# Four of seven Strassen products summed in one PSUM bank: a new product order and a fifth weight buffer in the first half of a fused transformer block

## The chip, the cores and the metric

The kernel runs on one core of one Trainium2 chip. The metric is the device time of one execution in microseconds; the time before is the median of three runs. Five engines work side by side, each with its own queue of instructions: TensorE (PE in the profile, its weight loads PEld), VectorE (DVE), ScalarE (ACT), GpSimd (POOL) and SyncE (SP), which issues most transfers. TensorE writes into PSUM, which has eight banks of 128 x 512 floats; VectorE and ScalarE read the banks from there.

## The reference

One layer on `x` of 2048 tokens by 1024 features, in float32:

```python
h    = rmsnorm(x, norm_g)
proj = einsum('bsd,de->bse', h, w_in)     # 1024 -> 4*512 + 4*512 + 2*1024 = 6144 columns
q, k, v, z_att, gb, gc, u, z_conv, g_att, g_conv = split(proj)
att    = chunked_rel_attention(q, k, v, rel_bias)      # 8 heads of 64; own chunk of 64 and 8 before
y_att  = (att * silu(z_att)) @ w_att_out
y_conv = (gb * causal_conv3(gc * u) * silu(z_conv)) @ w_conv_out
m   = sigmoid(g_att) * y_att + sigmoid(g_conv) * y_conv
x   = x + m @ w_out
out = rmsnorm(x, final_norm_g)
```

The change lies in `proj`, the large product of 2048 x 1024 by 1024 x 6144.

## The kernel before

**Tiles.** The tokens are taken in two halves of 1024 (two blocks of 512 columns each; the kernel holds everything transposed, features on partitions). The 6144 output columns are 24 pairs of 128-column tiles. One pair of one half is a 2 x 2 block product (output tiles by token blocks, with the 1024 features cut in two), and it is made by the Strassen-Winograd scheme with seven block products in place of eight. They bear the numbers 1 to 7. The tuple `ORDER` (L36) sets in which order they are made: 1, 2, 6, 5, 7, 4, 3. Each product sums over four tiles of 128 features, and each of these is done in three passes (`passes`, L132 to L137), because weights and activations are split into a high and a low part: high by high (L135), high by low (L136), low by high (L137). A product is therefore twelve matmuls of 128 x 512, into one PSUM bank.

**Operands.** `operand_steps` (L348 to L362) makes the seven activation operands of a half, four tiles each: an add for operand 6 (L354), a subtract for 4 (L356) and for 5 (L360), or the block itself, and then a split (`split_pair`, L125 to L130): ScalarE casts the high part (L128), VectorE subtracts it to get the low part (L129). In the names of the profile `t40h` is the high part of operand 4, tile 0. `operand` (L375 to L399) makes the weight operand of one product in the same way: up to three sums on VectorE (L390 to L396), then `split_into` with ScalarE's cast (L122) and VectorE's subtract (L123). Its tile `wc` comes from the pool `wr` of four buffers. The first half also stores each one to DRAM; the second half loads it back. Weight operands are made two products ahead of their use in the first half and three ahead in the second (`ahead`, L753). The raw weights are loaded a pair ahead (`load_raw`, L370 to L373, called at L749).

**Sums of the products.** The results of a pair are four blocks, c11, c12, c21, c22. With `u` and `v` as running sums, the code at L774 to L801 does this after each product, reading its bank once or twice: ScalarE copies product 1 into `u` (L776); VectorE makes c11 = u + product 2 (L780), u += product 6 (L784), v = u + product 5 (L787), c22 = v + product 7 (L791), u += product 7 (L792), c21: u += product 4 (L796), c12: v += product 3 (L800). That is seven adds and one copy per pair. Scratch tiles `u`, `v`, `c` come from the pool `ep` of ten buffers. Each finished block goes to a handler of its kind (L402 to L499): a gate gets a tanh on ScalarE (L404) and is stored; a q or k block is split again, ScalarE's cast `hi` (L410) and VectorE's subtract (L411); a v block is transposed by TensorE into a bank `vt` (L433) and cast out of it by ScalarE (`vst`, L440) and VectorE; z and the short convolution have their own.

**PSUM.** The pool `ps_d` has three banks; products, plain products, `vt` and the spread norm `rb` take turns in it. The other five belong to the attention's pools `ps_s`, `ps_t` and `ps_m`, opened at the start of the program (L99).

**Order of the work.** The first three pairs of the first half (`PLAIN`) are done plainly, in twelve accumulations L686 to L727, while x is still being normalised: their banks are `ps_p`, and `scaled` (L636 to L639) frees a bank by multiplying it with 1/rms (L638) on VectorE. The order of that part is the order in which it is written. Then the main loop (L741 to L822) goes through the list of (pair, product) steps `seq`. From there on a scheduler arranges each engine's instructions by their dependences and their places in the program, so that they do not stand simply in the order of the code. The last pairs of the first half and the first of the second are interleaved product by product (`together`, L584); beside them the second half's activation operands are made. Early in the second half `wo_steps` (L549 to L578) prepares the output weights `xw` on VectorE (L570 to L574). After that the attention of all heads (L177 to L259) is interleaved with the rest of the second half, and the two closing projections follow.

Of the kernel before, what the change touches and what calls it, by code (L numbers as in the profile page):

```python
# [34 lines left out]

ORDER = (1, 2, 6, 5, 7, 4, 3)  # L36
NPAIR = 24
# [3 lines left out]
def block_kernel(ctx, tc, xb, xt, wp_in, wy, wo, bias, ng, fg, cw, cb, out):  # L41
# [89 lines left out]

    def passes(ps, w, rhs, cs=slice(0, CH), first=True, last=True):  # L132

        for k, (rh, rl) in enumerate(rhs):
            nc.tensor.matmul(ps, lhsT=w[:, 0, k, :], rhs=rh[:, cs], start=(first and k == 0), stop=False)  # L135
            nc.tensor.matmul(ps, lhsT=w[:, 0, k, :], rhs=rl[:, cs], start=False, stop=False)  # L136
            nc.tensor.matmul(ps, lhsT=w[:, 1, k, :], rhs=rh[:, cs], start=False, stop=(last and k == len(rhs) - 1))  # L137

# [156 lines left out]
    def inverse(y, make):  # L295

        ps = dbank("rb")
        spread(ps, y, 4)
        rb = make("rb")
        nc.scalar.copy(rb, ps)  # L300
        return rb
# [98 lines left out]


    def ev_gate(i, d):  # L402
        def ev(g, c, t):
            nc.scalar.activation(t, t, AF.Tanh, scale=0.5)  # L404
            nc.scalar.dma_start(gate_d[i][d][g], t)
        return ev

    def parts(t):
        hi = e("hi")
        nc.scalar.copy(hi.bitcast(F32R), t)  # L410
        nc.vector.tensor_sub(t.bitcast(F32R), t, hi)  # L411
        return hi, t
# [15 lines left out]
    def ev_v(pr):  # L428
        def ev(g, c, t):
            def turn():  # L430
                ps = dbank("vt")
                for b in range(4):
                    nc.tensor.transpose(out=ps[:, b * P:(b + 1) * P], in_=t[:, b * P:(b + 1) * P], identity=ident)  # L433
                defer(0, lambda: split(ps))
# [28 lines left out]
    def conv_pair(b):  # L463
# [21 lines left out]
        def ev_cu(g, c, t):  # L485
            if c in got:
                conv(c, got.pop(c), t)
            else:
                got[c] = t

# [96 lines left out]

    both = [(i, k) for i in (6, 5, 7, 4, 3) for k in range(2)]
    ending = [(1, 0), (2, 0), (6, 0), (1, 1), (2, 1), (6, 1), *both[2:]]
# [151 lines left out]
    for s, (p, i) in enumerate(seq):  # L741
        half = p // NPAIR
        n = names.index(p)
        if due and due[0] <= s:
            due.pop(0)
            next(turned)
        if half == 0 and i == 1 and n + 1 < NPAIR:
            for k in range(2):
                load_raw(names[n + 1], k)  # L749
        elif i == 1 and n in (NPAIR, *range(NPAIR + 2, NPAIR + 1 + PLAIN)):  # L750
            for k in range(2):
                load_raw(names[max(n, NPAIR + 1) + 1], k)
        ahead = 3 if half else 2  # L753
        while nw < min(len(seq), s + ahead + 1):
            operand(*seq[nw])
            nw += 1
        if half == 0 and len(built) < 7 and s:
            built.append(next(steps))
        if n == 5 and i == 1:
# [3 lines left out]
            x1 = norm_steps(1)  # L763
        if half == 0 and 8 <= n < 22 and i in (2, 5, 4):
# [4 lines left out]
        ps = dbank("ps_d")  # L769
        passes(ps, wops.pop((p, i)), [ops[half, i, j] for j in range(4)])  # L770
        tick()
        ev = evs[p % NPAIR]
        g0, g1 = 2 * half, 2 * half + 1
        if i == 1:  # L774
            u = e("u")
            nc.scalar.copy(u, ps)  # L776
            uv[p] = [u, None]
        elif i == 2:
            t = e("c11")
            nc.vector.tensor_add(t, uv[p][0], ps)  # L780
            ev[0](g0, 0, t)
        elif i == 6:
            u = uv[p][0]
            nc.vector.tensor_add(u, u, ps)  # L784
        elif i == 5:
            v = uv[p][1] = e("v")
            nc.vector.tensor_add(v, uv[p][0], ps)  # L787
        elif i == 7:
            u, v = uv[p]
            t = e("c22")  # L790
            nc.vector.tensor_add(t, v, ps)  # L791
            nc.vector.tensor_add(u, u, ps)  # L792
            ev[1](g1, 1, t)
        elif i == 4:
            u = uv[p][0]
            nc.vector.tensor_add(u, u, ps)  # L796
            ev[1](g0, 0, u)
        else:
            v = uv.pop(p)[1]
            nc.vector.tensor_add(v, v, ps)  # L800
            ev[0](g1, 1, v)  # L801
        if n == NPAIR - 1:
# [9 lines left out]
        if n == NPAIR + 1 + PLAIN and i == 3:  # L812
            for _ in mixed:
                pass
            first.close()
            att = ExitStack()
            ab = attention(att.enter_context(tc.tile_pool(name="ab", bufs=1, side="right")))
# [303 lines left out]
```

## Time and profile before

| | |
|---|---|
| runs of before | 1537.36, 1541.26, 1545.34 us; median 1541.26 |
| profiled execution | 1537.43 us, span of the trace 1535.7 us |
| mean granted TensorE clock | 0.995 |
| memory traffic | 408.32 MB by DMA, 266 GB/s; 251.67 MB read from HBM, 155.19 MB written |

How to read the profile: it is one execution, and `L135` is line 135 of the kernel. Busy time counts an instruction from its start to its end; since matmuls are pipelined and their ends are modelled, the pace of TensorE is read from the distance of starts, or from how many matmuls a stretch holds. In the timeline a row is start, duration, engine, line, operation, output and inputs, and in brackets the idle time before it and what ended that. In a group's row stand busy time, mean nanoseconds of one, and the idle time before the group with its main releaser. The waits are rows of engine, waiting tile and line, releaser, then microseconds in all, their count, and the longest. Row pieces such as `x119` are counts.

### The profile page before, as it was taken

To read this page: it belongs to the slowest core of one execution; us is meant where nothing else is said; L and a number is where in the kernel's file an instruction comes from. 1 tells how busy PE (TensorE), PEld (TensorE's weight loads), DVE (VectorE), ACT (ScalarE), POOL (GpSimd) and SP (SyncE) were. 2 spreads that over 40 slices of the span, in tenths; PEclk is the share of its full clock that TensorE was granted. 3 is DMA by queue.
4 is the path that set the end of the run, shared out by engine and by line. 5 is a ranking of instruction groups with operands and counts; after the bars stand their busy time and mean duration, and the time that the engine had idled before them with its cause. 6 is when DMAs were issued, how large, how long until landed. Compare 5 with 4: busy or idle time off the path is not lost.

```text
span 1535.7 us, 21757 instructions
## 1 busy us (share of the span) xinstructions
PE 1493.8 (97%) x7300; PEld 1247.1 (81%) x7300; DVE 1108.6 (72%) x2140; ACT 714.5 (47%) x1314; POOL 164.0 (11%) x310
## 2 busy tenths in 40 slices
PE   8899999999999999999999999999999999999997
PEld 6678888888777778888888888888888888888885
DVE  7977789797668774666666767676755578777787
ACT  6353353443335333555566656666665223423252
POOL 0000000000000001233222223222220000010000
PEclk9999999999999999999999999999999999999999
DMA  5288999988988984999898777878888944877442
GB/s 206 76 287 310 343 350 326 360 324 290 334 301 277 318 315 149 336 342 337 299 295 278 236 259 235 264 240 267 293 273 300 337 116 163 297 253 234 149 157 110
DMA packets 168750, 408.32 MB, mean 266 GB/s; under 512 B 21056, under 2 KB 41536, under 8 KB 168640
## 3 DMA queue, kind: packets, MB, share of 16 engines
q1 hardware_dynamic: 137152, 316.74, 59.4%
q0 software_dynamic: 22272, 73.42, 14.6%
q10 hardware_dynamic: 9216, 16.78, 2.9%
q8 instruction: 58, 0.95, 0.3%
q14 instruction: 52, 0.43, 0.1%
HBM read 251.67 MB, written 155.19 MB: 265 GB/s over the span
## 4 chain that ended last, share of the span: by engine, by line
PE 79%; DVE 10%; DMA 5%; issue 3%; ACT 3%; POOL 0%; SPq 0%; ACTq 0%; DVEq 0%; POOLq 0%
PE ps_d L137 19%; PE ps_d L135 19%; PE ps_d L136 19%; PE ps_w L953 6%; PE ps_d L953 4%; PE po L228 4%; PE ps_s L190 3%; PE ps_t L210 3%; DMA wc<-wc 1%; DMA vv<-v 1%; DVE ptl L216 1%; DMA xw<-wo 1%; DVE ps_s L196 1%; DVE xs L304 1%; ACT pr L200 1%
## 5 line engine op out<-in xcount | busy, mean ns | idle before, releaser
L158 POOL DMA_DIRECT2D q<-q x128 | 66.9, 528 | 675.2 <-DVE wc L123 598.4
L200 ACT ACTIVATE pr<-ps_s,nmax 128x640 f32<-128x640 f32 (+4 forms) x128 | 93.4, 730 | 96.9 <-DVE nmax L196 96.2
L196 DVE CUSTOM_DVE_ANT_0 ps_s<-ps_s,bs 128x640 f32<-128x640 f32 (+4 forms) x128 | 95.3, 744 | 53.9 <-PE ps_s L190 53.2
L122 ACT CAST wc<-wraw 128x512 fp32r<-128x512 f32 x120 | 73.4, 620 | 105.9 <-PE ps_d L137 80.1
L202 ACT ACTIVATE pr<-pr,rs 128x640 f32<-128x640 f32 (+4 forms) x128 | 97.8, 764 | 27.4 <-DVE rs L201 27.3
L190 PE MATMUL ps_s<-kk,q 128*128 128x320 f32 (+1 forms) x448 | 98.0, 335 | 2.8 <-ACT pr L200 2.6
L216 DVE TENSOR_TENSOR ptl<-ps_t,pth 128x640 fp32r<-128x640 f32 (+4 forms) x128 | 94.2, 736 | 7.5 <-ACT pth L215 6.9
L137 PE MATMUL ps_d<-mid,wy 128*128 128x512 f32 x256 | 99.6, 389 | 0.0
L135 PE MATMUL ps_d<-mid,wy 128*128 128x512 f32 x256 | 99.6, 389 | 0.0
L136 PE MATMUL ps_d<-mid,wy 128*128 128x512 f32 x256 | 99.6, 389 | 0.0
L215 ACT CAST pth<-ps_t 128x640 fp32r<-128x640 f32 (+4 forms) x128 | 80.1, 626 | 41.3 <-PE ps_t L210 40.3
L123 DVE TENSOR_TENSOR wc<-wraw,wc 128x512 fp32r<-128x512 f32 x120 | 81.8, 686 | 10.1 <-ACT wc L122 9.9
L210 PE MATMUL ps_t<-ident,pr 128*128 128x128 f32 x560 | 83.9, 276 | 1.0 <-DVE ptl L216 0.5
L228 PE MATMUL po<-pth,vv 128*128 128x256 f32 x336 | 79.1, 271 | 2.6 <-DMA vv<-v 2.5
L228 PE MATMUL po<-ptl,vv 128*128 128x256 f32 x336 | 78.1, 281 | 0.0
L190 PEld LDWEIGHTS ps_s<-kk,q 128*128 128x128 f32 x448 | 67.0, 190 | 7.6 <-ACT pr L200 7.2
L210 PEld LDWEIGHTS ps_t<-ident,pr 128*128 128x128 f32 x560 | 63.3, 141 | 11.1 <-DVE ptl L216 2.0
L953 PE MATMUL ps_w<-wo,lefth 128*128 128x512 f32 x224 | 69.9, 393 | 0.0
L228 PEld LDWEIGHTS po<-pth,vv 128*128 128x128 f32 x336 | 63.8, 190 | 6.0 <-issue 2.6
L228 PEld LDWEIGHTS po<-ptl,vv 128*128 128x128 f32 x336 | 63.8, 190 | 2.4 <-DVE ptl L216 0.2
L137 PEld LDWEIGHTS ps_d<-mid,wy 128*128 128x128 f32 x256 | 48.1, 188 | 10.1
L136 PEld LDWEIGHTS ps_d<-mid,wy 128*128 128x128 f32 x256 | 48.1, 188 | 10.0
(383 smaller groups left out, 4174.2 us busy)
## 6 DMA issues: line engine op xcount, KB each, us to landing
wc<-wc SPq DMA_DIRECT2D x294, 512.0 KB, 4.8
wraw<-wp_in SPq DMA_DIRECT2D x54, 512.0 KB, 6.1
q<-q POOLq DMA_DIRECT2D x128, 128.0 KB, 4.9
gl<-gate SPq DMA_DIRECT2D x64, 256.0 KB, 3.2
mid<-mid SPq DMA_DIRECT2D x64, 256.0 KB, 5.3
wor<-wo SPq DMA_DIRECT2D x56, 256.0 KB, 5.2
bs<-bias POOLq DMA_DIRECT2D x32, 320.0 KB, 7.5
gate<-c ACTq DMA_DIRECT2D x34, 256.0 KB, 5.2
```

The lines of the kernel that those rows point to most:

```text
L123: nc.vector.tensor_sub(w[:, 1], src, w[:, 0].bitcast(F32))
L135: nc.tensor.matmul(ps, lhsT=w[:, 0, k, :], rhs=rh[:, cs], start=(first and k == 0), stop=False)
L136: nc.tensor.matmul(ps, lhsT=w[:, 0, k, :], rhs=rl[:, cs], start=False, stop=False)
L137: nc.tensor.matmul(ps, lhsT=w[:, 1, k, :], rhs=rh[:, cs], start=False, stop=(last and k == len(rhs) - 1))
L190: nc.tensor.matmul(ps[:, i, :m], lhsT=q[s][:, g * P:(g + 1) * P], rhs=kk[:, k1 - n + i * m:k1 - n + (i + 1) * m], start=(s == 0), stop=(s ...
L196: nc.vector.tensor_tensor_reduce(out=view, in0=view, in1=bv, scale=-0.125, scalar=3.0e38, op0=ALU.add, op1=ALU.min, accum_out=nmax)
L200: nc.scalar.activation(out, view, AF.Exp, bias=nmax, scale=-1.0, accum_out=rs)
L202: nc.scalar.activation(pr[:, :n], pr[:, :n], AF.Identity, scale=rs)
L210: nc.tensor.transpose(out=ps[:, j * P:(j + 1) * P], in_=pr[:, j * P:(j + 1) * P], identity=ident)
L216: nc.vector.tensor_sub(lo[:, js, qs], src, hi[:, js, qs].bitcast(F32))
L228: nc.tensor.matmul(ps[:, (g0 + a) * P:(g0 + b) * P], lhsT=vv[:, g0 + j, :], rhs=s[:, j, a * P:b * P], start=(i == 0 and s is pt[0]), stop= ...
L953: nc.tensor.matmul(ps, lhsT=lhs[:, gs], rhs=rhs, start=(not onto and j == n == 0), stop=(j == 3 and n == 2), skip_group_check=onto)
```

## The change

The change rearranges the first half's Strassen products and the PSUM banks they use.

- `ORDER` becomes 1, 2, 6, 7, 4, 5, 3, in both halves.
- In the first half, products 1, 6, 5 and 3 of a pair go into one shared bank (pool `ps_c`, two banks). Product 1 starts it; 6, 5 and 3 add onto what is there (`onto`). Between them ScalarE copies the bank out: after product 1 and after product 6 into a `u`, after product 5 into `v`. After product 3 the bank itself is c12, and it is passed to the handler as it is. Product 7 has a pool of its own, `ps_h`, of two banks, which is held until it is read twice. Products 2 and 4 stay in `ps_d`. VectorE's adds are now four per pair: c11 after 2, u after 7, c21 after 4, and v += product 7 after 5, which makes c22. ScalarE's copies are three.
- The second half keeps a bank per product and sums in the new order: u after 6, w = u + product 7, c21 = w + product 4, then w and u each plus product 5, u plus product 3.
- The weight pool `wr` has five buffers in place of four, the scratch pool `ep` eight in place of ten. Weight operands are made three products ahead in both halves.
- The attention's pools are opened only when the attention begins; until then their five banks are `ps_m` (one), `ps_c` and `ps_h`. Two of the v transposes and `rb` use `ps_m`.
- In the first half the steps of neighbouring pairs interleave: 6, 7, 4, 5 of a pair, then products 1 and 2 of the next pair, then 3.
- The raw weights' load is issued after `operand` of the step, and the small work (norm steps of the second half, bias) after the product, not ahead of it.

```diff
-ORDER = (1, 2, 6, 5, 7, 4, 3)
+ORDER = (1, 2, 6, 7, 4, 5, 3)
...
-    wr = pool("wr", 4)
-    ep = pool("ep", 10)
+    wr = pool("wr", 5)
+    ep = pool("ep", 8)
     ps_d = pool("ps_d", 3, space=PSUM)
     banks = ExitStack()
-    ps_s, ps_t, ps_m = (banks.enter_context(tc.tile_pool(name=name, bufs=1, space=PSUM)) for name in ("ps_s", "ps_t", "ps_m"))
+    ps_m = banks.enter_context(tc.tile_pool(name="ps_m", bufs=1, space=PSUM))
+    ps_c = banks.enter_context(tc.tile_pool(name="ps_c", bufs=2, space=PSUM))
+    ps_h = banks.enter_context(tc.tile_pool(name="ps_h", bufs=2, space=PSUM))
...
-    def passes(ps, w, rhs, cs=slice(0, CH), first=True, last=True):
+    def passes(ps, w, rhs, cs=slice(0, CH), first=True, last=True, onto=False):
...
+            nc.tensor.matmul(ps, lhsT=w[:, 0, k, :], rhs=rh[:, cs], start=(first and not onto and k == 0), stop=False, skip_group_check=onto)
...
+    def own(src):
+        return src if src.space != PSUM else e("c12")
+
+    def copied_out(src):
+        t = own(src)
+        if t is not src:
+            nc.scalar.copy(t, src)
+        return t
...
-    def parts(t):
-        hi = e("hi")
-        nc.scalar.copy(hi.bitcast(F32R), t)
-        nc.vector.tensor_sub(t.bitcast(F32R), t, hi)
+    def parts(src):
+        hi, t = e("hi"), own(src)
+        nc.scalar.copy(hi.bitcast(F32R), src)
+        nc.vector.tensor_sub(t.bitcast(F32R), src, hi)
...
-                ps = dbank("vt")
+                ps = bank("vt") if g < 2 else dbank("vt")
...
-    seq = [(p, i) for p in mid0 for i in ORDER]
+    seq = [(mid0[0], 1), (mid0[0], 2)]
+    for p, nxt in zip(mid0, names[PLAIN + 1:]):
+        seq += [*((p, i) for i in (6, 7, 4, 5)), (nxt, 1), (nxt, 2), (p, 3)]
...
+        ahead = 3
+        while nw < min(len(seq), s + ahead + 1):
+            operand(*seq[nw])
+            nw += 1
         if half == 0 and i == 1 and n + 1 < NPAIR:
             for k in range(2):
                 load_raw(names[n + 1], k)
-        ahead = 3 if half else 2
-        while nw < min(len(seq), s + ahead + 1):
-            operand(*seq[nw])
-            nw += 1
...
+        onto = half == 0 and i in (6, 5, 3)
+        if onto:
+            ps = uv[p][0]
+        elif half == 0 and i in (1, 7):
+            ps = (ps_c if i == 1 else ps_h).tile([P, CH], F32, tag="b", name="ps_c")
+        else:
+            ps = dbank("ps_d")
+        passes(ps, wops.pop((p, i)), [ops[half, i, j] for j in range(4)], onto=onto)
...
+        elif half == 0:
+            if i == 6:
+                u = uv[p][2] = e("u")
+                nc.scalar.copy(u, ps)
+            elif i == 7:
+                u = uv[p][2]
+                nc.vector.tensor_add(u, u, ps)
+                uv[p][1] = ps
+            elif i == 4:
+                u = uv[p][2]
+                nc.vector.tensor_add(u, u, ps)
+                ev[1](g0, 0, u)
+            elif i == 5:
+                v = e("v")
+                nc.scalar.copy(v, ps)
+                nc.vector.tensor_add(v, v, uv[p][1])
+                ev[1](g1, 1, v)
+            else:
+                uv.pop(p)
+                ev[0](g1, 1, ps)
```

What this does to the queues is seen at two places. The first is ScalarE's queue at the last q and k pair of the first half. Before, with `wc_4059`, `wc_4078` and `wc_4099` the weights of products 7, 4 and 3, and `hi_4119` the cast of c22, which is finished after product 7:

```order
L122 CAST wc_4034<-s1_4007 128x512
L410 CAST hi_4056<-c11_4054 128x512
L122 CAST wc_4059<-wraw_3836 128x512
L410 CAST hi_4119<-c22_4116 128x512
L122 CAST wc_4078<-wraw_3836 128x512
L122 CAST wc_4099<-wraw_3834 128x512
```

After, at the same pair, with `wc_3942`, `wc_3969` and `wc_3989` the weights of products 7, 4 and 5, `u_3940` the copy of product 1, `hi_3985` the cast of the previous pair's c12 out of the shared bank, and `u_4007` the copy after product 6:

```order
L124 CAST wc_3942<-wraw_3756 128x512
L793 COPY u_3940<-ps_c_3922 128x512
L124 CAST wc_3969<-wraw_3756 128x512
L124 CAST wc_3989<-s1_3911 128x512
L422 CAST hi_3965<-u_3940 128x512
L422 CAST hi_3985<-ps_c_3758 128x512
L803 COPY u_4007<-ps_c_3922 128x512
```

The cast of product 4's weights stood behind a cast of the sum that product 7 completes; it now stands between the copy of product 1 and the weights of product 5.

The second place is VectorE's queue at the start, between the multiplies by 1/rms that free the plain products' banks. Before, `t50l` to `t53l` are the low parts of activation operand 5:

```order
L638 TENSOR_TENSOR c_1108<-ps_p_1006,rb_925 128x512
L360 TENSOR_TENSOR t1_1141<-xs_547,xs_533 128x512
L129 TENSOR_TENSOR t50l_1144<-t1_1141,t50h_1143 128x512
L360 TENSOR_TENSOR t1_1147<-xs_547,xs_533 128x512
L129 TENSOR_TENSOR t51l_1150<-t1_1147,t51h_1149 128x512
L360 TENSOR_TENSOR t1_1153<-xs_547,xs_533 128x512
L129 TENSOR_TENSOR t52l_1156<-t1_1153,t52h_1155 128x512
L360 TENSOR_TENSOR t1_1159<-xs_547,xs_533 128x512
L129 TENSOR_TENSOR t53l_1162<-t1_1159,t53h_1161 128x512
L638 TENSOR_TENSOR c_1165<-ps_p_1063,rb_852 128x512
```

After, from the same multiply on, with the low parts of operands 7 and 4 and, in the last row, the split of the weights of the first Strassen product:

```order
L654 TENSOR_TENSOR c_1108<-ps_p_1006,rb_925 128x512
L131 TENSOR_TENSOR t70l_1142<-xs_544,t70h_1141 128x512
L131 TENSOR_TENSOR t71l_1146<-xs_544,t71h_1145 128x512
L131 TENSOR_TENSOR t72l_1150<-xs_544,t72h_1149 128x512
L131 TENSOR_TENSOR t73l_1154<-xs_544,t73h_1153 128x512
L654 TENSOR_TENSOR c_1157<-ps_p_1063,rb_852 128x512
L358 TENSOR_TENSOR xs_539<-xs_539,xs_533 128x512
...
L131 TENSOR_TENSOR t43l_1203<-xs_539,t43h_1202 128x512
L654 TENSOR_TENSOR c_1206<-ps_p_1116,rb_852 128x512
L125 TENSOR_TENSOR wc_1210<-wraw_558,wc_1210 128x512
```

Four bare splits now stand between the first and the second multiply, where four subtracts and four splits stood; four subtracts and splits stand between the second and the third, and the first weights' split comes behind those. Lines 124, 125, 130, 131, 422, 654, 793, 803 and 814 of the changed kernel are the lines 122, 123, 128, 129, 410, 638, 776 and the two new copies after products 6 and 5.

More of the change, by code (lines that the diff above doesn't have):

```diff
@@ L130, in split_pair @@
         return hi, lo
-    def passes(ps, w, rhs, cs=slice(0, CH), first=True, last=True):
+    def passes(ps, w, rhs, cs=slice(0, CH), first=True, last=True, onto=False):
         for k, (rh, rl) in enumerate(rhs):
-            nc.tensor.matmul(ps, lhsT=w[:, 0, k, :], rhs=rh[:, cs], start=(first and k == 0), stop=False)
-            nc.tensor.matmul(ps, lhsT=w[:, 0, k, :], rhs=rl[:, cs], start=False, stop=False)
-            nc.tensor.matmul(ps, lhsT=w[:, 1, k, :], rhs=rh[:, cs], start=False, stop=(last and k == len(rhs) - 1))
+            nc.tensor.matmul(ps, lhsT=w[:, 0, k, :], rhs=rh[:, cs], start=(first and not onto and k == 0), stop=False, skip_group_check=onto)
+            nc.tensor.matmul(ps, lhsT=w[:, 0, k, :], rhs=rl[:, cs], start=False, stop=False, skip_group_check=onto)
+            nc.tensor.matmul(ps, lhsT=w[:, 1, k, :], rhs=rh[:, cs], start=False, stop=(last and k == len(rhs) - 1), skip_group_check=onto)
     def attention(ab):
@@ L295, in inverse @@
     def inverse(y, make):
-        ps = dbank("rb")
+        ps = bank("rb")
         spread(ps, y, 4)
@@ L488, in ev_cu @@
             else:
-                got[c] = t
+                got[c] = copied_out(t)
         def gated(g, c, t):
@@ L746, in block_kernel @@
             next(turned)
+        if i == 1 and n in (NPAIR, *range(NPAIR + 2, NPAIR + 1 + PLAIN)):
+            for k in range(2):
+                load_raw(names[max(n, NPAIR + 1) + 1], k)
+        ahead = 3
+        while nw < min(len(seq), s + ahead + 1):
+            operand(*seq[nw])
+            nw += 1
         if half == 0 and i == 1 and n + 1 < NPAIR:
@@ L763, in block_kernel @@
             x1 = norm_steps(1)
-        if half == 0 and 8 <= n < 22 and i in (2, 5, 4):
+        ev = evs[p % NPAIR]
+        g0, g1 = 2 * half, 2 * half + 1
+        onto = half == 0 and i in (6, 5, 3)
[6 more added lines that the diff above has]
+        passes(ps, wops.pop((p, i)), [ops[half, i, j] for j in range(4)], onto=onto)
+        tick()
+        if i == 1:
+            u = e("u")
+            nc.scalar.copy(u, ps)
+            uv[p] = [ps, None, u]
+        elif i == 2:
+            u = uv[p][2]
+            t = u if half == 0 else e("c11")
+            nc.vector.tensor_add(t, u, ps)
+            ev[0](g0, 0, t)
+        elif half == 0:
+            if i == 6:
+                u = uv[p][2] = e("u")
+                nc.scalar.copy(u, ps)
+            elif i == 7:
[3 more added lines that the diff above has]
+            elif i == 4:
+                u = uv[p][2]
+                nc.vector.tensor_add(u, u, ps)
[8 more added lines that the diff above has]
+                ev[0](g1, 1, ps)
+        elif i == 6:
+            u = uv[p][2]
+            nc.vector.tensor_add(u, u, ps)
+        elif i == 7:
+            w = uv[p][1] = e("w")
+            nc.vector.tensor_add(w, uv[p][2], ps)
+        elif i == 4:
+            t = e("c21")
+            nc.vector.tensor_add(t, uv[p][1], ps)
+            ev[1](g0, 0, t)
+        elif i == 5:
+            _, w, u = uv[p]
+            nc.vector.tensor_add(w, w, ps)
+            nc.vector.tensor_add(u, u, ps)
+            ev[1](g1, 1, w)
+        else:
+            u = uv.pop(p)[2]
+            nc.vector.tensor_add(u, u, ps)
+            ev[0](g1, 1, u)
+        if half == 0 and 8 <= n < 22 and i in (2, 7, 4):
             next(x1, None)
@@ L768, in block_kernel @@
             nbias += 1
[L769 to L801, printed above, removed]
         if n == NPAIR - 1:
@@ L815, in block_kernel @@
             first.close()
+            banks.close()
+            ps_s, ps_t, ps_m = (banks.enter_context(tc.tile_pool(name=name, bufs=1, space=PSUM)) for name in ("ps_s", "ps_t", "ps_mm"))
             att = ExitStack()
```

15 lines of the change are left out of this document (7 added, 8 removed).

## The prediction

> **What bounds the kernel now.** I read the page first, for the busy shares and the chain of work that ended last.
>
> ```profile
> PE 1493.8 (97%) x7300; PEld 1247.1 (81%) x7300; DVE 1108.6 (72%) x2140; ACT 714.5 (47%) x1314; POOL 164.0 (11%) x310
> PE 79%; DVE 10%; DMA 5%; issue 3%; ACT 3%; POOL 0%; SPq 0%; ACTq 0%; DVEq 0%; POOLq 0%
> ```
>
> TensorE is the bound. The change removes no matmul, so all it can win is time in which TensorE does not run at its pace. Next I read the busy time by stretches (columns: TensorE, weight load, VectorE, ScalarE, GpSimd, each with its count, granted clock, DMA share).
>
> ```profile
> 50.00:90.00 40.00, 30.81 (x119) 24.06 (x118) 36.11 (x59) 18.88 (x33) 0.00 (x0) 0.91 0.34 111
> 120.00:400.00 280.00, 280.00 (x1241) 231.91 (x1240) 228.46 (x418) 112.27 (x201) 0.00 (x0) 1.00 0.89 329
> 400.00:440.00 40.00, 36.12 (x160) 28.77 (x158) 25.62 (x41) 11.89 (x24) 0.00 (x0) 1.00 0.84 303
> 440.00:480.00 40.00, 39.62 (x183) 32.08 (x184) 28.47 (x52) 17.08 (x36) 0.00 (x0) 1.00 0.95 319
> 480.00:520.00 40.00, 34.92 (x143) 27.32 (x142) 38.75 (x65) 20.82 (x37) 0.00 (x0) 0.96 0.80 283
> 560.00:600.00 40.00, 38.02 (x168) 31.16 (x168) 25.01 (x39) 14.63 (x24) 0.24 (x1) 1.00 0.43 157
> 720.00:1160.00 440.00, 435.67 (x2545) 380.47 (x2544) 300.30 (x607) 273.84 (x476) 114.62 (x214) 1.00 0.82 268
> ```
>
> From 120 to 400 us, which holds most pairs of the first half, TensorE is never idle: 1241 matmuls in 280 us, one every 0.2256 us, so a product of twelve takes 2.71 us and 40 us hold 177 matmuls. What the other stretches lack against 177 is the loss: 58 matmuls from 50 to 90 (13.1 us), 17 from 400 to 440 (3.9), 34 from 480 to 520 (7.7), 9 from 560 to 600 (2.0); 440 to 480 has 0.4 us of idle time. Together 27.1 us are lost in the first half and its transition. The list of TensorE's waits from 50 to 600 us says for whom.
>
> ```profile
> PE ps_p L135 <- DVE c L638: 9.2, 3, 4.6
> PE ps_d L137 <- DVE wc L123: 5.5, 4, 3.1
> PE ps_d L135 <- ACT wc L122: 3.5, 3, 1.9
> PE ps_d L135 <- DVE u L784: 2.0, 1, 2.0
> ```
>
> And the timeline of TensorE, at those waits:
>
> ```profile
> 60.35 0.47 PE L135 MATMUL ps_p<-rawh,w 128*128 128x512 f32 x1 [2.48 <-DVE c L638]
> ...
> 76.25 0.80 PE L135 MATMUL ps_p<-rawh,w 128*128 128x512 f32 x1 [4.61 <-DVE c L638]
> ...
> 77.27 0.63 PE L137 MATMUL ps_p<-rawh,w 128*128 128x512 f32 x1
> 77.70 0.63 PE L135 MATMUL ps_p<-rawh,w 128*128 128x512 f32 x1
> ...
> 85.59 0.50 PE L135 MATMUL ps_p<-rawh,w 128*128 128x512 f32 x1 [2.09 <-DVE c L638]
> ...
> 87.31 0.63 PE L137 MATMUL ps_p<-rawh,w 128*128 128x512 f32 x1
> 87.73 0.63 PE L135 MATMUL ps_p<-rawh,w 128*128 128x512 f32 x1
> ...
> 92.79 0.39 PE L135 MATMUL ps_d<-t10h,wc 128*128 128x512 f32 x1
> ...
> 414.08 0.50 PE L135 MATMUL ps_d<-t40h,wc 128*128 128x512 f32 x1 [1.95 <-ACT wc L122]
> ...
> 436.21 0.50 PE L137 MATMUL ps_d<-t40h,wc 128*128 128x512 f32 x1 [1.53 <-DVE wc L123]
> ...
> 491.23 0.50 PE L135 MATMUL ps_d<-t70h,wc 128*128 128x512 f32 x1 [1.31 <-ACT wc L122]
> ...
> 501.29 0.50 PE L137 MATMUL ps_d<-t40h,wc 128*128 128x512 f32 x1 [3.14 <-DVE wc L123]
> ...
> 565.13 0.47 PE L135 MATMUL ps_d<-t40h,wc 128*128 128x512 f32 x1 [1.98 <-DVE u L784]
> ```
>
> So only eight places matter, and at most of them a weight split comes late, not a sum. After two of the start's waits matmuls follow each other at 0.43 instead of 0.23 us for a while: the start's 13.1 us are 9.2 of waiting and 3.9 of such slow stretches.
>
> **Part by part: the adds and copies.** In the first half each pair loses three of its seven VectorE adds and gains two ScalarE copies.
>
> ```profile
> L787 DVE TENSOR_TENSOR v<-u,ps_d 128x512 f32<-128x512 f32 x21 | 14.4, 685 | 13.0 <-PE ps_d L137 13.0
> L776 ACT COPY u<-ps_d 128x512 f32<-128x512 f32 x21 | 12.2, 583 | 12.6 <-PE ps_d L137 12.2 <-ACT v L404 0.4
> ```
>
> By 0.69 and 0.58 us that is 3 x 0.69 = 2.1 us per pair off VectorE, about 43 us over 21 pairs, and 21 x 2 x 0.58 = 24 us onto ScalarE. VectorE has 51 us to spare from 120 to 400, and TensorE never waits there: both terms are nothing in that stretch. The cover for the copies is that products 6, 5 and 3, which add into the shared bank, each come two products (5.4 us) after the one whose sum is copied out; a copy of 0.58 us fits unless ScalarE is held up for more than 4.8 us. For the first pair there is only one product between 1 and 6. If the cover is gone, TensorE stands for the excess.
>
> **The start.** VectorE's and ScalarE's rows there:
>
> ```profile
> 75.52 0.68 DVE L638 TENSOR_TENSOR c<-ps_p,rb 128x512 f32<-128x512 f32 x1
> ...
> 78.14 0.69 DVE L129 TENSOR_TENSOR t50l<-t,t50h 128x512 fp32r<-128x512 f32 x1 [1.35 <-ACT t50h L128]
> ...
> 80.17 0.69 DVE L129 TENSOR_TENSOR t51l<-t,t51h 128x512 fp32r<-128x512 f32 x1 [0.74 <-ACT t51h L128]
> ...
> 84.85 0.68 DVE L638 TENSOR_TENSOR c<-ps_p,rb 128x512 f32<-128x512 f32 x1
> ```
>
> Between the multiply that frees one plain bank (75.52) and the next (84.85) stand four rounds of subtract, cast, split for operand 5, 2.03 us each (78.14 to 80.17). In the new order four bare splits of operand 7 stand there, so the second multiply starts at 76.2 + 1.35 of waiting for a cast + 4 x 0.69 = 80.3 and ends at 81.0: the 2.09 us wait at 85.59 goes, and with it half of the slow stretches, 4.0 us together. The 2.48 and 4.61 us waits hang on rows that stay. But four such rounds (operand 4) now stand ahead of the split of the first product's weights: 81.0 + 8.1 + a multiply and the split, 1.4, is 90.5, where TensorE, which began that product at 92.79, is 4.0 us earlier, at 88.8. It waits 1.7 us (bounds 0 and 4.0). Term: -2.3 us, between -4.0 and 0.
>
> The trace throttles after a wait of 2.09 us. [...]
>
> **From 400 to 480.** The wait at 414.08 is made by queue order, not by load:
>
> ```profile
> 412.17 0.69 DVE L791 TENSOR_TENSOR c<-v,ps_d 128x512 f32<-128x512 f32 x1
> 412.89 0.62 ACT L410 CAST hi<-c 128x512 fp32r<-128x512 f32 x1 [7.02 <-DVE c L791]
> 413.41 1.66 ACT L122 CAST wc<-wraw 128x512 fp32r<-128x512 f32 x3
> ```
>
> ScalarE holds the cast of product 4's weights behind the cast of a finished sum that waits for product 7, the one just before: 0.69 + 0.62 + 0.62 = 1.93, and 1.95 was waited. In the new ScalarE order that weight cast stands behind product 1's copy, three products ahead of need: gone. The wait at 436.21 (an add of product 7 ahead of the split) goes with the fifth buffer's extra product of lead, 2.71 us. In their place I see in the new order three tight spots at the v pairs: a weight cast behind the cast out of a transpose that TensorE does just before, a weight cast behind a copy that waits for such a transpose, and a split behind three weight sums.
>
> ```profile
> 439.71 0.37 ACT L440 CAST vst<-vt 128x256 fp32r<-128x256 f32 x1 [5.03 <-PE vt L433]
> ```
>
> The first is 0.37 + 0.62 plus a quarter of a microsecond at the low part, 1.3; the second 0.58 + 0.62 = 1.2; the third about 0.4. Term: 4.3 lost before, 2.9 after, -1.4 us (bounds -4.3 and +1.5, if each doubles).
>
> **From 480 to 520.** Here VectorE is full (38.75 of 40 us), since the second half's operands are made beside the last two pairs, and the splits come late. Two pairs lose six adds, 4.1 us of VectorE; weights come a product earlier; operand 5 is needed two products later. That exceeds the 3.14 and 1.31 us waits. I leave 1.0 us: -6.7 us (bounds -7.7 and 0, as the order in this crowded place is new).
>
> **From 560 to 600.** VectorE stood 4.6 us before a row of the output weights, with the add that frees a bank behind it:
>
> ```profile
> 562.25 0.69 DVE L570 TENSOR_TENSOR xw<-xw 128x512 f32<-128x512 f32 x1 [4.62 <-DMA xw<-wo]
> ```
>
> The new order spreads these rows between other adds, but the load can be as late: half of it, -1.0 us (bounds -2.0 and +1.0).
>
> **The rest at nothing.** The raw weights' load is issued after the splits of the step and behind them in SP's queue. It now has four products (10.8 us) where five were, and lands in 6.1 us at the median:
>
> ```profile
> wraw<-wp_in SPq DMA_DIRECT2D x38, 512.0 KB, 6.1
> ```
>
> Two scratch tiles fewer can make a copy wait for a store; stores hide behind the same two products. The small work that is moved behind the product (norm steps, bias) has no reader near. The second half keeps its counts, and from 720 to 1160 only 4.3 us are idle, so order changes there are worth within 4 us either way; I take 0.
>
> **Sum.** -2.3 - 1.4 - 6.7 - 1.0 = -11.4 us. The profiled execution took 1537.4 us, so 1526 for one like it; the median of the runs is 3.8 us higher at 1541.3, and from it 1530.
>
> **The rivals.** *The copies become the wait.* Sharing a bank makes TensorE wait wherever ScalarE is late with a copy. For it: the 7.02 us for which ScalarE stood before a cast at 412.89, and that q, k and v pairs keep such casts, now behind adds of product 4 and ahead of the copy of product 5. Against it: those casts wait for a product already done two products before the bank is needed. It decides once a copy ends later than 5.4 us after its product. If two points in each of the six q, k and v pairs then cost the 1.95 us of 414.08, that is 23.4 us, +12.0 net: 1553. [...]
>
> *The waits only move.* They came from the order in which weight casts and sums stand in ScalarE's and VectorE's queues, which is drawn up anew; new tight spots could return what 400 to 600 gives. Only the start's term is left: 1539. For it: three such spots are visible already. Against it: all weights now come one product earlier.
>
> *More goes than I count.* If the start loses its wait for weights too (-4.0), and 400 to 480 (-4.3), 480 to 520 (-7.7) and 560 to 600 (-2.0) lose everything: -18.0, 1523, or below if the slow stretch after 76.25 also shrinks. For it: the fifth buffer works at each of these places.
>
> **How the numbers follow.** 0.52 for the forecast (its own range 1523 to 1537), 0.15 for more, 0.24 for waits that move, 0.09 for late copies. A measurement of this kernel can tell about 0.5%, 7.7 us, from no change: 1533.6. Of the forecast's chance 0.37 lies below that. Faster: 0.37 + 0.15 = 0.52. Slower takes most of the last rival, 0.07. The same is 0.41. The range reaches from 1517, under the third rival, to 1546, over the second with the second half's 4 us and some scatter of the runs; it leaves out most of the first.
>
> **What would show it.** Right: full TensorE from 120 to 400, no wait at the product 4 that waited at 414.08, at least 165 matmuls where 480 to 520 had 143, a start with two waits for plain banks instead of three and one for the first weights. Wrong: waits of TensorE at products 6, 5 or 3 for ScalarE's copies; weight waits of over 5 us in sum between 400 and 600; a second half with more than 8 us idle from 720 to 1160.

## The result and the profile after

The changed kernel takes 1525.52 us (median of five runs, 1523.16 to 1526.19), beside 1540.23 us for the kernel before (five runs); the ratio is 0.9904 with a 95% interval of 0.9876 to 0.9932. A second series, with more runs of both on one chip, gave 1524.42 and 1537.15 us: 0.9911 (0.9893 to 0.9928). The forecast was 1530, 11 us less; the runs say 13 to 15 us less, and between the two profiled executions (1537.43 and 1525.53 us) it is 11.9.

The page of the profile after, busy shares and the chain of work that ended last:

```profile
PE 1490.2 (98%) x7300; PEld 1246.4 (82%) x7300; DVE 1071.2 (70%) x2077; ACT 732.5 (48%) x1358; POOL 163.6 (11%) x310
PE 83%; DVE 8%; issue 3%; DMA 3%; ACT 2%; POOL 0%; SPq 0%; ACTq 0%; DVEq 0%; POOLq 0%
```

VectorE has 63 instructions fewer, three in each of the 21 pairs, and ScalarE 44 more: the 42 copies, and two of finished blocks whose handler needs them out of the bank. That is 37 us off VectorE and 18 onto ScalarE, less than the 43 and 24 that had been counted. The chain's share on VectorE and on DMA went to TensorE. Next the busy time by the stretches that were shown of before (TensorE, weight load, VectorE, ScalarE, GpSimd, each with its count, granted clock, DMA share and rate).

```profile
50.00:90.00 40.00, 31.60 (x131) 24.81 (x129) 32.36 (x54) 17.49 (x31) 0.00 (x0) 0.96 0.33 108
120.00:400.00 280.00, 280.00 (x1241) 231.90 (x1240) 206.83 (x377) 126.26 (x233) 0.00 (x0) 1.00 0.94 337
400.00:440.00 40.00, 38.93 (x177) 31.75 (x176) 21.53 (x37) 13.18 (x27) 0.00 (x0) 1.00 0.80 284
440.00:480.00 40.00, 38.75 (x180) 31.75 (x179) 27.17 (x50) 22.04 (x46) 0.00 (x0) 1.00 0.90 309
480.00:520.00 40.00, 37.13 (x155) 29.69 (x154) 34.23 (x58) 18.93 (x35) 0.00 (x0) 0.96 0.89 315
560.00:600.00 40.00, 40.00 (x178) 33.15 (x177) 21.12 (x33) 13.98 (x23) 7.57 (x14) 1.00 0.50 152
720.00:1160.00 440.00, 438.01 (x2567) 383.83 (x2567) 299.91 (x608) 279.25 (x480) 111.85 (x209) 1.00 0.83 268
```

From 120 to 400 us nothing changed for TensorE: 1241 matmuls in both profiles, with 22 us less of VectorE and 14 more of ScalarE beside them. The gains lie where the prediction had put the losses. TensorE's idle time from 400 to 480 falls from 4.3 to 2.3 us; 480 to 520 holds 155 matmuls in place of 143, still 22 short of full; 560 to 600 is full. The second half, from 720 to 1160, has 2.0 us of idle time in place of 4.3. What TensorE still waits for shows in its timeline from 50 to 600 us; these are the rows with a wait, not neighbours, and in the end the row behind the last of them:

```profile
59.99 0.47 PE L137 MATMUL ps_p<-rawh,w 128*128 128x512 f32 x1 [2.49 <-DVE c L654]
75.60 0.50 PE L137 MATMUL ps_p<-rawh,w 128*128 128x512 f32 x1 [4.32 <-DVE c L654]
89.98 0.50 PE L137 MATMUL ps_c<-t10h,wc 128*128 128x512 f32 x1 [1.60 <-ACT wc L124]
435.99 0.50 PE L137 MATMUL ps_d<-t20h,wc 128*128 128x512 f32 x1 [1.07 <-ACT wc L124]
467.86 0.50 PE L137 MATMUL ps_c<-t10h,wc 128*128 128x512 f32 x1 [1.25 <-ACT wc L124]
493.24 0.50 PE L137 MATMUL ps_c<-t30h,wc 128*128 128x512 f32 x1 [0.54 <-ACT v L814]
509.75 0.77 PE L137 MATMUL ps_d<-t20h,wc 128*128 128x512 f32 x1 [2.33 <-DMA wc<-wc]
510.32 0.63 PE L138 MATMUL ps_d<-t20l,wc 128*128 128x512 f32 x1
```

Two waits for plain banks where three were, one for the first weights, two at the v pairs, and two new ones: 0.54 us for ScalarE's copy of `v` and 2.33 us for a weight load of the second half, with a slow stretch behind it (matmuls 0.43 us apart). Why the load is late stands in SP's queue, L474 being the store of a z block and L383 the loads of the second half's weights:

```profile
497.30 0.42 SPq L383 DMA_DIRECT2D wc<-wc  x1
502.31 0.32 SPq L474 DMA_DIRECT2D z<-sz  x1
502.68 0.91 SPq L375 DMA_DIRECT2D wraw<-wp_in  x2
503.69 0.38 SPq L383 DMA_DIRECT2D wc<-wc  x1
```

SP issues nothing for 4.6 us. The list of SP's own waits from 485 to 515 us names whom it stands for:

```profile
SPq L474 <- DVE sz L468: 10.9, 5, 4.5
```

The store needs a product that VectorE makes at 501.59 us, behind the splits of operand 4 of the second half, the last of which starts at 500.39:

```profile
501.59 0.69 DVE L468 SCALAR_TENSOR_TENSOR sz<-sz,v 128x512 f32<-128x512 f32 x1
```

The weight load behind it in SP's queue is issued at 503.69 and lands when TensorE has already stood 2.33 us for it.

### The profile page after: what moved, and what is told of

The parts are those of the page before. It is cut to its first block, busy times and chain, and to the rows that moved or that the text cites. A ratio compares the mean times of both kernels' runs of the same rounds, so it can differ in the third digit from the quotient of the medians.

```text
span 1523.8 us, 21646 instructions
## 1 busy us (share of the span) xinstructions
PE 1490.2 (98%) x7300; PEld 1246.4 (82%) x7300; DVE 1071.2 (70%) x2077; ACT 732.5 (48%) x1358; POOL 163.6 (11%) x310
## 4 chain that ended last, share of the span: by engine, by line
PE 83%; DVE 8%; issue 3%; DMA 3%; ACT 2%; POOL 0%; SPq 0%; ACTq 0%; DVEq 0%; POOLq 0%
PE ps_d L137 14%; PE ps_d L139 14%; PE ps_d L138 14%; PE ps_w L997 6%; PE ps_c L137 6%; PE ps_c L138 6%; PE ps_c L139 6%; PE ps_d L997 4%; PE po L230 4%; PE ps_s L192 4%; PE ps_t L212 3%; DMA vv<-v 1%; DVE xs L306 1%; DVE ptl L218 1%; DVE ps_s L198 0%
## 5 line engine op out<-in xcount | busy, mean ns | idle before, releaser
L137 PEld LDWEIGHTS ps_d<-mid,wy 128*128 128x128 f32 x256 | 48.1, 188 | 11.4 <-ACT wy L124 1.7
```

## The experiments

The theory after the result: in the first half TensorE is held up by two things, weights that come late and sums that come late, and each part of the change removes one of them; copies out of the shared bank cost nothing because two products cover them. Rivals: it is the fewer adds on VectorE alone; or the copies cost time that something else wins back. All medians stand beside the kernel before on the same chip (1537.89, 1538.64 and 1537.15 us in the three series). The changed kernel itself was run again only in the third series, so a trial of the first two that differs from it by 2 or 3 us is judged by its profile and not by its time. The load of the raw weights and the small work that were moved, and the attention's later pools, were not tried alone.

### A store in another queue

```diff
-            defer(1, lambda: store(z_d[pr][g], t))
+            defer(1, lambda: (nc.gpsimd.dma_start if g < 2 else store)(z_d[pr][g], t))
```

> The changed kernel with one edit: the first half's stores of the z blocks are issued from GpSimd's queue, not from SP's. Theory (what is left of the loss from 480 to 520 us is one wait of 2.33 us at product 2 of the second half's first pairs, because SP stood 4.5 us before a z store that waits for VectorE, with the weight loads behind it; and the slow stretch after the wait, 4.42 us for a product in place of 2.71): the wait at 509.75 us goes, 2.33 + 1.7 = about 4 us faster than the changed kernel, 1521. Rival (the load is late because the DMA engines are full there, 294 GB/s): the wait stays above 1.5 us and the time within 1 us of the changed kernel's.

Measured: 1523.54 us, 0.9908 (0.9885 to 0.993), where 1521 was expected. The wait at 509.75 is gone, but the wait for product 1 at 467.86 grew to 3.13 us, with a slow stretch (matmuls 0.43 us apart). ScalarE's queue there tells why (the kernel of this trial):

```profile
468.61 0.59 ACT L803 COPY u<-ps_c 128x512 f32<-128x512 f32 x1 [3.15 <-DMA z<-sz]
469.09 1.14 ACT L124 CAST wc<-wraw 128x512 fp32r<-128x512 f32 x2
```

The copy out of the shared bank waits for a store: its scratch tile is the one that a z block is still being stored from, and the weight cast stands behind it. The transfers' rows from 440 to 480 us, of this trial and of the changed kernel (the last number is the time from issue to landing):

```profile
z<-sz POOLq DMA_DIRECT2D x1, 256.0 KB, 4.5
```

```profile
z<-sz SPq DMA_DIRECT2D x1, 256.0 KB, 2.2
```

From GpSimd's queue that store took 2.3 us longer (one transfer each). So the theory on the load holds, and the trial found a second thing: with eight scratch tiles a slower store reaches TensorE by way of the copy.

### The fifth buffer alone, and all but the fifth buffer

```diff
-    wr = pool("wr", 4)
-    ep = pool("ep", 10)
+    wr = pool("wr", 5)
+    ep = pool("ep", 8)
...
-        ahead = 3 if half else 2
+        ahead = 3
```

These lines on the kernel before are the first trial, and the same lines taken back in the changed kernel are the second.

> The kernel before with the fifth weight buffer alone (wr 5, ep 8, weights three products ahead in both halves); products, banks, adds and order as before. Theory (the waits from 400 to 520 us are weights that come late, and one more product of lead, 2.71 us, takes most of them): the waits at 414.08, 436.21, 491.23 and 501.29 us shrink from 7.9 us to under 3, with the slow stretch behind the longest, 5 to 8 us faster than before, 1532 to 1535. Rival (VectorE's seven adds per pair make the weights late, so only the shared bank helps): under 2 us faster, the wait at 501.29 still over 2 us.

> The changed kernel with the old weight buffers (wr 4, ep 10, weights two products ahead in the first half); shared bank, order and start as changed. Theory (lead of the weights): waits for weights between 400 and 520 us grow from 5.7 us to 9 or more, 4 to 8 us slower than the changed kernel, 1530 to 1534. Rival (fewer adds on VectorE are what helps): within 2 us of the changed kernel, 1524 to 1528.

Measured: the buffer alone 1532.91 us, 0.9975 (0.9957 to 0.9993), as expected; all but the buffer 1536.95, 0.999 (0.9976 to 1.0003), no gain that can be told, and 3 us above the range that was expected. The longest of TensorE's waits from 90 to 600 us, first with the buffer alone:

```profile
PE ps_d L135 <- ACT sz L453: 3.9, 1, 3.9
PE ps_d L135 <- ACT wc L122: 1.2, 2, 1.0
PE ps_d L135 <- DVE vst L441: 1.1, 1, 1.1
PE ps_d L135 <- DVE c L780: 0.9, 1, 0.9
```

Then with all but the buffer:

```profile
PE ps_c L137 <- ACT wc L124: 3.7, 2, 1.9
PE ps_d L139 <- DVE wc L125: 3.6, 5, 1.0
PE ps_d L137 <- DMA wc<-wc: 2.5, 2, 2.1
PE ps_c L139 <- DVE wc L125: 1.5, 1, 1.5
```

With the buffer, the waits for weights (`wc`) shrink from 9.0 us before to 1.2, but TensorE then stands for banks that are not yet read (`sz`, `vst`, `c`). The longest of these waits is put down to `sz`, which reads no bank. VectorE's last read of a bank there is an add of product 7; it ends at 498.26 us, the matmul starts at 498.40, and VectorE had not paused for the 9 us before. So the sum was late, and not a scratch tile. Without the buffer it is the other way round: 8.8 us of waits for weight casts and splits, none for the shared banks. So neither part does it alone. Of the 12.7 us of the whole, the buffer by itself gives 5.0 and the rest by itself 0.9; apart they come to less than half.

### The start

Two trials. On the kernel before, operand 7 is made ahead of operand 5 in the first half:

```diff
-        for i in ORDER:
+        for i in (ORDER if half else (1, 2, 6, 7, 5, 4, 3)):
```

> The kernel before with one edit: in the first half activation operand 7 is made before operand 5, the products stay in the old order. Theory (the start's gain is that four bare splits stand between the multiplies that free the plain banks): the 2.09 us wait at 85.59 and the slow stretch behind it go, a wait of about 1.6 us for the first weights comes, and the first Strassen product starts 2.6 us earlier; all later waits as before: 2 to 3 us faster than before in the profile. Rival (the start gains from the new banks or the interleaved steps): no change, three waits for plain banks.

Measured: 1538.42 us, 1.0002 (0.9986 to 1.0018). In the profile the first Strassen product starts at 89.87 us in place of 92.79, as in the changed kernel (89.98), so the start's gain comes from the order of these operands. But the medians show nothing of it: in the profile about 1 us is given back from 480 to 620 us, where a wait for a load of weights (1.44 us) and one for the attention (1.09 us) have appeared, and what is left, 1.8 us where 2 to 3 were expected, is under what the runs' scatter lets one see.

On the changed kernel, one operand less is made during the plain products:

```diff
-        if q > 5 and len(built) < 5:
+        if q > 5 and len(built) < 4:
```

> The changed kernel with four activation operands instead of five made during the plain products, so that operand 4 (four subtracts, casts and splits) no longer stands whole ahead of the split of the first Strassen product's weights. Theory (the 1.60 us wait at 88.38 comes from those rounds): this wait goes, the start is 1.6 us earlier, 1524. Rival (the raw weights or the free buffer are late, not VectorE): the wait stays; or the rounds only move and make product 4's operand late, a wait near 100 us.

Measured: 1523.18 us, 0.9908 (0.9885 to 0.9932). TensorE's waits from 50 to 110 us are down to the two plain banks:

```profile
PE ps_p L137 <- DVE c L654: 7.2, 2, 4.7
```

The 1.60 us for the first weights is gone, and no wait for operand 4 has come.

### The copies

First the cover is taken away: each pair's products are written together, and four matmuls are left between product 5 and product 3. The order of the last two pairs and the raw weights' load are fitted to it; the main lines:

```diff
-    seq = [(mid0[0], 1), (mid0[0], 2)]
-    for p, nxt in zip(mid0, names[PLAIN + 1:]):
-        seq += [*((p, i) for i in (6, 7, 4, 5)), (nxt, 1), (nxt, 2), (p, 3)]
+    seq = [(p, i) for p in mid0 for i in ORDER]
...
```

> The changed kernel with each pair's seven products written together (1, 2, 6, 7, 4, 5, 3) in the first half, not with the next pair's 1 and 2 ahead of 3 (the raw weights of the last pair are loaded a step earlier). In the built order four matmuls of the next product now stand between products 5 and 3, 0.9 us where 5.4 us were. Theory (the copies cost nothing because two products cover them): with 0.9 us of cover a copy of 0.58 us fits only where ScalarE is free at once; TensorE waits for copies after product 5 at several of the 21 pairs, 2 to 8 us slower than the changed kernel, 1528 to 1533. Rival (ScalarE is half idle, copies never matter): within 1 us of the changed kernel.

Then the load is doubled: the copies after products 6 and 5 are made twice.

```diff
                 nc.scalar.copy(u, ps)
+                nc.scalar.copy(u, ps)
...
                 nc.scalar.copy(v, ps)
+                nc.scalar.copy(v, ps)
```

> The changed kernel with the ScalarE copy after product 6 and the one after product 5 made twice in each pair of the first half, 42 copies of 0.58 us more, 24 us of ScalarE. Theory (two products, 5.4 us, cover a copy): no cost from 120 to 400 us, at most 2 us more where weight casts wait behind copies, from 400 to 520; 1525 to 1528. Rival (the copies are on the path): up to 24 us slower, 1535 or more, with waits of TensorE for ScalarE's copies in every pair.

Measured: without the cover 1530.66 us, 0.9951 (0.993 to 0.9972), 5 to 6 slower; with doubled copies 1526.0, 0.9928 (0.9907 to 0.9949), 0.5 to 1.6 slower than the changed kernel's two medians (2.6 to 3.7 by the ratios to the kernel before) for 24 us of extra copying. TensorE's waits for the doubled copies, from 90 to 600 us:

```profile
PE ps_c L137 <- ACT v L816: 1.3, 2, 1.0
PE ps_c L137 <- ACT u L804: 1.2, 1, 1.2
```

The longest waits of that stretch without the cover:

```profile
PE ps_c L137 <- ACT wc L124: 5.9, 3, 3.1
PE ps_c L137 <- ACT v L815: 3.0, 4, 1.4
PE ps_c L137 <- ACT u L794: 1.8, 2, 1.5
```

Without the cover the copies (`v` after product 5, `u` after product 1) hold TensorE for 4.8 us where they held it for 0.54, and the waits for weight casts, without the 1.59 us at the start, grew from 2.3 to 4.3. With the cover, twice the copying holds it for 2.5 us. So a copy is nearly free because of where products 3 and 6 stand, not because ScalarE is half idle.

### The order alone, and the change without the shared bank

On the kernel before, only the order of products becomes 1, 2, 6, 7, 4, 5, 3, summed in both halves as the changed kernel's second half does; buffers, banks and lead as before.

```diff
-ORDER = (1, 2, 6, 5, 7, 4, 3)
+ORDER = (1, 2, 6, 7, 4, 5, 3)
...
+        elif i == 7:
+            w = uv[p][1] = e("w")
+            nc.vector.tensor_add(w, uv[p][0], ps)
...
+        elif i == 5:
+            u, w = uv[p]
+            nc.vector.tensor_add(w, w, ps)
+            nc.vector.tensor_add(u, u, ps)
+            ev[1](g1, 1, w)
```

> The kernel before with the new order of products alone (1, 2, 6, 7, 4, 5, 3, with the second half's sums in both halves); four weight buffers, two products of lead, ten scratch tiles, own banks, no interleaving. Theory: the start gains 2.3 to 2.6 us as in the trial with operand 7 ahead of 5, the second half 1 to 2 us as in the changed kernel, and the waits for weights from 400 to 520 us stay or move (7.9 us before): 1534 to 1537. Rival (the order itself puts the weights of the late products earlier): those waits fall below 4 us, 1530 or less.

On the changed kernel, products 1, 6, 5 and 3 each start a bank of their own in `ps_c`, and VectorE makes seven sums per pair beside one copy on ScalarE.

```diff
-        onto = half == 0 and i in (6, 5, 3)
-        if onto:
-            ps = uv[p][0]
-        elif half == 0 and i in (1, 7):
-            ps = (ps_c if i == 1 else ps_h).tile([P, CH], F32, tag="b", name="ps_c")
+        onto = False
+        if half == 0 and i in (1, 6, 5, 3, 7):
+            ps = (ps_h if i == 7 else ps_c).tile([P, CH], F32, tag="b", name="ps_c")
...
```

> The changed kernel without the shared bank: in the first half each product starts its own bank (1, 6, 5 and 3 take turns in the two banks of ps_c), and VectorE makes the sums as in the second half, seven adds... six and one copy; new order, interleaving and five weight buffers stay. Theory (VectorE's adds are off the path except where it is full, 480 to 520 us): no loss from 120 to 400, within 3 us of the changed kernel in all but that stretch, 1526 to 1531. Rival (the sums in PSUM are what makes the change work): waits for sums or weights all through the first half, back to 1535 or more.

Measured: the order alone 1535.23 us, 0.999 (0.9976 to 1.0005); without the shared bank 1531.12, 0.9958 (0.9942 to 0.9974), 6.7 us slower than the changed kernel, just above the range that was expected. The order alone keeps the weight waits (9.0 us from 400 to 520, as before), and it gives the second half's gain whole; its stretch from 720 to 1160 us:

```profile
720.00:1160.00 440.00, 438.02 (x2564) 383.63 (x2563) 300.71 (x612) 277.57 (x480) 114.21 (x213) 1.00 0.81 270
```

438.02 us busy, as in the changed kernel (438.01); with the buffer alone it is 435.85, beside 435.67 before. Without the shared bank, two stretches lose (busy time by stretches, then the two waits from 90 to 600 us that the changed kernel doesn't have; two others are under 0.4 us):

```profile
120.00:400.00 280.00, 277.00 (x1223) 228.46 (x1223) 229.47 (x419) 112.65 (x202) 0.00 (x0) 1.00 0.93 333
480.00:520.00 40.00, 36.47 (x150) 29.59 (x149) 39.26 (x66) 21.43 (x38) 0.00 (x0) 0.91 0.83 295
```

```profile
PE ps_c L137 <- ACT sz L467: 3.5, 1, 3.5
PE ps_c L137 <- ACT u L791: 2.3, 1, 2.3
```

From 480 to 520 VectorE is full again (39.26 of 40 us) and a bank of `ps_c` is read late, as the theory says: its last reader is an add of product 5, which ends at 500.17, and the matmul that waited 3.53 us starts at 500.31.

```profile
499.49 0.68 DVE L811 TENSOR_TENSOR u<-u,ps_c 128x512 f32<-128x512 f32 x1
```

The 2.3 us at 212 us were not expected. There a copy stood behind a square of the second half's norm that waited 2.51 us for its load and a tanh that waited 0.34 us for a store; both have scratch tiles, of which these sums hold more. That the tiles are the reason is argued, not shown. The trial keeps eight scratch tiles and gives the four products two banks; with more of either it was not tried, so the 6.7 us are the worth of the shared bank in this arrangement.

### Two waits taken away

The z stores of the second token block are put off by two products, so that they stand behind the weight loads in SP's queue.

```diff
-            defer(1, lambda: store(z_d[pr][g], t))
+            defer(3 if g == 1 else 1, lambda: store(z_d[pr][g], t))
```

> The changed kernel with the stores of the second token block's z tiles put off by two products, so that they stand behind the weight loads in SP's queue; still SP's. Theory (the 2.33 us wait at product 2 comes from SP's queue; the first trial in GpSimd's queue only moved it, since the slower stores held scratch tiles and the copy after product 6 at 468.61 us waited for one): the wait for the second half's weights goes, and with it the slow stretch, while the copy at 466.70 us isn't held; 4 us faster than the changed kernel, 1521 to 1522. Rival (scratch tiles held longer by the late stores stop a copy in the same stretch): another wait of 1.5 us or more between 490 and 515 us and less than 1.5 us gained.

Measured: 1522.43 us, 0.9901 (0.9882 to 0.992); in the profile the wait at 509.75 and its slow stretch are gone, 4.2 us at that place (from product 1 at 504.55 to product 6 at 514.17 in the changed kernel, 9.62 us; here 5.44). Then this edit together with the four operands at the start:

> The changed kernel with both edits that each took away one wait: four operands made during the plain products, and the z stores of the second block put off by two products. Theory (the two waits are independent): 1.6 + 4.2 = 5.8 us faster than the changed kernel, about 1520. Rival (a gain at the start is given back at the next place where a load is late): no better than either alone, 1522 to 1523.

> The changed kernel once more, as the base for the others on this chip: 1525.5 by its first five runs, 12 to 15 us faster than before.

Measured: both edits 1518.5 us, 0.9875 (0.9856 to 0.9894); the changed kernel again 1524.42. The two gains add up, 5.9 us beside 5.8 expected, between two kernels of one series. The combined kernel's stretch from 480 to 520 us and its waits from 50 to 600:

```profile
480.00:520.00 40.00, 39.48 (x173) 32.04 (x172) 33.83 (x56) 18.93 (x34) 0.00 (x0) 1.00 0.89 329
```

```profile
PE ps_p L137 <- DVE c L654: 7.1, 2, 4.6
PE ps_c L137 <- ACT wc L124: 1.2, 1, 1.2
PE ps_d L137 <- ACT wc L124: 1.1, 1, 1.1
PE ps_c L137 <- ACT v L814: 0.5, 1, 0.5
```

173 matmuls where the changed kernel has 155 and full is 177. This version beats both kernels.

## Why the prediction was right, point by point

- *TensorE bounds, and the adds taken from VectorE are worth nothing from 120 to 400 us.* Right: 1241 matmuls before and after. The trial without the shared bank loses 3.0 us there, so this holds for the two kernels and not for any arrangement of the sums.
- *The start, -2.3.* Right: the first Strassen product starts at 89.98 in place of 92.79, -2.8; the new wait for its weights was to be 1.7 us and is 1.60. The trials with operand 7 and with four operands show both halves of that step. Of the 2.8 us, 0.36 were there before the first of these waits (60.35 and 59.99), which the prediction has no reason for. Had the 2.09 us wait cost itself alone, TensorE would have been at 90.7, behind the weights at 90.5, and the term -2.1. What speaks for the slow stretch is that TensorE was ready at 88.38, 4.4 us earlier.
- *400 to 480, -1.4.* Right in its places: the waits at 414.08 and 436.21 are gone, the first two tight spots cost 1.07 and 1.25 us (1.3 and 1.2 forecast), the third nothing. 4.3 us lost became 2.3, so -1.9.
- *480 to 520, -6.7.* This is the step that failed: "I leave 1.0 us". 5.0 are left (22 matmuls), so the term is -2.7. The weights of the first half did come a product earlier. What was overlooked is the second half's weights: a load, behind a z store in SP's queue, behind VectorE; with its slow stretch it cost 4.2 of the 5.0. The prediction looked at ScalarE's and VectorE's queues there, and at SP's only for the raw weights. With the store put off, the stretch gains the 6.7 that were forecast (143 to 173 matmuls, 6.8 us).
- *560 to 600, -1.0.* The whole 2.0 went, and why is open. The rows of the output weights do stand spread between adds, and VectorE's longest wait for their load is 2.95 us in place of 4.62. But with the order alone TensorE still waits 2.30 us at 560.73, with all but the buffer 0.37 and 0.92 us, with the buffer alone 0.89 and 0.56 us, so none of these parts alone is the reason; without the shared bank it does not wait there, so the shared bank is not either.
- *The second half, 0.* It gained 2.3 us, within the 4 us allowed. The order of products does it, as the trial with the order alone shows; the prediction gave no reason and took none.
- *Two scratch tiles fewer hide behind the same products.* True in the changed kernel, but with little to spare: a store 2.3 us slower was enough to hold a copy.
- *The raw weights' load, 0.* Right for TensorE; VectorE, though, waits for raw weights 24.0 us from 90 to 600 where it waited 7.5.
- *From the profile to the median, +3.8.* An execution like the profiled one was forecast at 1526 and took 1525.53. The 3.8 us by which the runs of the kernel before lay above its profile were added for the changed kernel too, and there they are not: its median is 1525.52. So 1530 was 4.5 us too slow.
- *The signs.* 155 matmuls came where at least 165 were to show that it was right, and the 0.54 us at product 3 are a small case of the sign against it. The weight waits from 400 to 600, 4.65 us, stayed just under the 5 us that were to count as wrong.

The terms so read sum to -2.8 - 1.9 - 2.7 - 2.0 - 2.3 = -11.7, beside 11.9 between the profiles and 11.4 forecast: one term too large and four too small came out nearly even, and that is luck. The rival of late copies is refuted for this order by the doubled copies (2.5 us of such waits) and by 0.54 us of them in the changed kernel, and the trial without cover shows that it would have been the right worry for another order of steps. The rival of waits that only move was true at one place, the load at 509.75.

On the shared bank, the runs show what the kernel's waiting for the copy costs where copy and accumulation follow each other closely: 3.0 us at four waits after product 5 without the cover.

## What to carry to other kernels

When an engine waits for late inputs and for late outputs by turns, a change that mends one of them shows little until the other is mended too (here 5.0 and 0.9 of 12.7 us); test both halves before giving one up. Sums in a PSUM bank were nearly free here only as long as other products stood between an accumulation and the next one (after product 5, 0.54 us of waits for copies with 5.4 us between, 3.0 us with 0.9), so the order of the products is part of the edit. And at a transition read the transfer queue as well: here a store that waited for the busy VectorE kept SP from issuing anything for 4.6 us, with a load of weights behind it.

## What the runs showed of the hardware

Whether an idle gap of 1.9 to 3.3 us makes TensorE slow afterwards is not settled by its length. Ahead of the same matmul at 60 us the idle time was 2.48 us, within 0.01, in all fourteen profiles; in ten the next matmuls came at full pace, in four (the buffer alone, the doubled copies, the late store, the order alone) seven or eight of them came 0.43 us apart, 1.5 to 1.8 us lost. The shortest gap with such a stretch behind it was 1.86 us (the doubled copies, at 470.18), the longest without one 3.25 us (the order alone, at 506.16). The wait for the second half's weights shows both faces. In the changed kernel, 2.33 us and a slow stretch:

```profile
509.75 0.77 PE L137 MATMUL ps_d<-t20h,wc 128*128 128x512 f32 x1 [2.33 <-DMA wc<-wc]
...
511.17 0.63 PE L137 MATMUL ps_d<-t21h,wc 128*128 128x512 f32 x1
511.60 0.63 PE L138 MATMUL ps_d<-t21l,wc 128*128 128x512 f32 x1
```

With four operands at the start, 2.17 us and none (the granted clock from 480 to 520 us is 0.96 in the first and 1.00 in the second):

```profile
508.27 0.47 PE L137 MATMUL ps_d<-t20h,wc 128*128 128x512 f32 x1 [2.17 <-DMA wc<-wc]
...
509.03 0.39 PE L137 MATMUL ps_d<-t21h,wc 128*128 128x512 f32 x1
509.26 0.39 PE L138 MATMUL ps_d<-t21l,wc 128*128 128x512 f32 x1
```

So a gap of much the same length did one thing or the other. This may also be why the kernel before, with more such waits, scatters more (1532 to 1545 us) than the changed one (1523 to 1526); that was not tested. For a sum by hand, an estimate from the 1.5 to 1.8 us above: such a gap carries about 1.7 us that may or may not be paid; once, after 2.75 us at 75.33 in the order alone, it was thirteen matmuls and nearly 3 us.
